# Softmax weights split on the query side and transposed by DMA in a two-layer GLA and dilated-attention trunk

## The chip, the cores and the metric

The kernel runs on one core of one Trainium2 chip. The metric is the device time of one execution in microseconds (us), as a median of several runs. All times below are us unless ns is written.

## What is computed

The reference runs two pre-norm residual layers over 2048 tokens of width 1024. Layer A mixes with gated linear attention, layer B with dilated window attention in three groups of six heads; both add a four-head attention into a memory of 256 tokens. The two places with a softmax are what matters here:

```python
def memory_attention(q, mem_n, w_memkv):          # 4 heads of 64, 256 memory tokens
    s = jnp.einsum('bthd,bnhd->bhtn', q, k).astype(jnp.float32) * (MEM_HEAD_DIM ** -0.5)
    p = jax.nn.softmax(s, axis=-1).astype(v.dtype)
    o = jnp.einsum('bhtn,bnhd->bthd', p, v)

def dilated_group(q, k, v, window, dilation):     # 6 heads of 128, blocks of 128 queries
    s = jnp.einsum('bphjqd,bphjkd->bphjqk', qb, kw).astype(jnp.float32) * (Dh ** -0.5)
    s = jnp.where(mask, s, -jnp.inf)              # own block and the one before it
    m = jnp.max(s, axis=-1, keepdims=True)
    p = jnp.exp(s - m)
    den = jnp.sum(p, axis=-1, keepdims=True)
    o = jnp.einsum('bphjqk,bphjkd->bphjqd', (p / den).astype(v.dtype), vw)
    lse = (m + jnp.log(den))[..., 0]
```

## The kernel before

Every product runs on TensorE (PE) in fp16 halves: a number is kept as a high half and a low half, and `mm3` (L164) makes three matmuls, high by high, high by low, low by high. The program is written in straight line; a scheduler sets the order on each engine, so code of one step stands between code of others. All DMAs are issued by SyncE (SP) on one queue.

Layer A has two loops over 16 blocks of 128 tokens. The first does the linear attention. The second does, for each block, `a2_q` (queries of the memory attention, its scores and its weighted sum, L612), `a2_gate` (96 matmuls of the gate path), `a2_branch` and `a2_out` (96 matmuls of the output projection) and `a2_h2`. Layer B runs over nine units (three pairs of heads, three groups). A unit projects queries and keys (`proj_qk`, eight tiles of 24 matmuls of 512 columns for each head), values (`proj_v`), and calls `attend` (L819) once for each of its two heads. Between and after the units stand `gate_item`s (24, L923), which join the three groups' outputs, and at the end comes the memory attention of layer B over 16 blocks (`mem_scores` one block ahead of `mem_pv`). An output projection closes the kernel.

The softmax path is the same in both places. Scores land in a PSUM bank with queries on partitions. VectorE (DVE) takes the maximum (L833 in `attend`, L243 in `mem_scores`), ScalarE (ACT) makes the exponentials into an fp32 tile in SBUF (L844, tile `pm`; L249, tiles `mp` and `mpt`). The weighted sum needs keys on partitions, so PE transposes each 128x128 block (L847; L161 in `split_T`), ACT copies the PSUM result to fp16 with the factor SP = 2**14 (L852, L262), DVE writes the remainder (L853, L263) and PE multiplies by the values (L165 to L167 into `ps_o`; L271 and L273). `attend` works on pairs of query blocks, eight pairs for each head. In it a pair has 2 to 4 blocks of weights to transpose: 31, 28 and 16 blocks for each head in the three groups, 450 in all; the two memory attentions have 8 for each token block, 256 in all. Tiles of the pool `bk` have two buffers, those of `gk` one. The staging tiles `stg` (pools `stg` and `sga`, one buffer each) hold raw weights while they are split.

Of the kernel before, what the change touches and what calls it, by code (L numbers as in the profile page):

```python
# [26 lines left out]
SQ = 2.0 ** -16  # L27
SP = 2.0 ** 14
NEG = -3.0e38
GROUPS = ((1, 16), (4, 4), (16, 1))  # L30
# [3 lines left out]
def trunk(ctx, tc, a, out):  # L34
# [23 lines left out]
    def bank(p_):  # L58
        return tl(p_, [P, 512], F32, p_.name)

# [1 line left out]
    def cload(name, shape, dt=F32, src=None):  # L62
# [93 lines left out]
    def split_T(src, n, emit):  # L156
        for k0 in range(0, n, 4):
# [15 lines left out]

# [1 line left out]
    def mem_kv(i, memT, spools):  # L175
# [26 lines left out]
    def load_mem(i, pl, invs, iq):  # L202
        kk = tl(pl, [P, 4, 256], F16, f"kk{i}")
        kl = tl(pl, [64, 4, 256], F16, f"kl{i}")
        vm = tl(pl, [P, 2, 512], F16, f"vm{i}")
        for hh in range(2):
            for dst, j in ((kk[0:64], 0), (kk[64:128], 0), (kl, 1)):
                SY.dma_start(dst.rearrange("p (r h) n -> p h r n", h=2)[:, hh],
                             kv_d[i][j, hh * 64:(hh + 1) * 64, :].rearrange("p (r n) -> p r n", r=2))
        SY.dma_start(vm, kv_d[i][2:4].rearrange("j p n -> p j n"))  # L210
        sc = col()
        V.tensor_scalar(out=sc, in0=iq, scalar1=invs[0], scalar2=0.125 / SQ, op0=ALU.mult, op1=ALU.mult)
        ov = col()
        V.tensor_scalar(out=ov, in0=invs[1], scalar1=1.0 / SP, scalar2=None, op0=ALU.mult)
        return kk, kl, vm, sc, neg_of(sc), ov
# [8 lines left out]

    def mem_scores(mem, q2, wk, tg):
        kk, kl, vm, sc, nsc, ov = mem
        qmT = tl(wk, [P, 512], F16, tg[0])
        t = tl(ps_tr, [P, 1024], F16, "ps_tr")
        for j in range(4):
            PE.transpose(t[:, j * P:(j + 1) * P], q2[:, j].rearrange("p a d -> p (a d)"), id16)  # L230
        V.tensor_copy(qmT, t[:, :512])
        den = tl(sp, [P, 4], F32, "mden")
        mx = tl(sp, [P, 4], F32, "mmx")
        ps = []
        for hh in range(2):
            s = bank(ps_g)
            for jj in range(2):
# [6 lines left out]
            V.tensor_scalar(out=m2, in0=m2, scalar1=nsc, scalar2=None, op0=ALU.mult)  # L244
            p_ = tl(wk, [P, 512], F32, tg[1 + hh])
            ps.append(p_)
            for jj in range(2):
                j = hh * 2 + jj
                A.activation(out=p_[:, jj * 256:(jj + 1) * 256], in_=s[:, jj * 256:(jj + 1) * 256],  # L249
                             func=AF.Exp, scale=sc, bias=m2[:, jj:jj + 1], accum_out=den[:, j:j + 1])  # L250
        return ps, den

    def mem_pv(mem, sd, om, po):
# [4 lines left out]
        for hh in range(2):  # L258
            pt = ps[hh].bitcast(F16).rearrange("p (a n) -> p a n", a=2)

            def emit2(k0, k1, t, pt=pt):
                A.activation(out=pt[:, 0, :], in_=t, func=AF.Copy, scale=SP)  # L262
                V.scalar_tensor_tensor(out=pt[:, 1, :], in0=t, scalar=SP, in1=pt[:, 0, :], op0=ALU.mult,  # L263
                                       op1=ALU.subtract)
            split_T(ps[hh], 4, emit2)
            for jj in range(2):
                j = hh * 2 + jj
                for m in range(2):
                    ts = slice((jj * 2 + m) * P, (jj * 2 + m + 1) * P)
                    vs = slice(m * 256 + j * 64, m * 256 + (j + 1) * 64)  # L270
                    PE.matmul(ov2[:, :, j * 64:(j + 1) * 64], pt[:, 0, ts], vm[:, :, vs], start=m == 0,  # L271
                              stop=False)
                    PE.matmul(ov2[:, 0, j * 64:(j + 1) * 64], pt[:, 1, ts], vm[:, 0, vs], start=False,  # L273
                              stop=m == 1)
# [37 lines left out]

    # =============== layer A ===============
    pa_ctx = ctx.enter_context(ExitStack())
# [284 lines left out]
    with ExitStack() as c2:  # L599
# [12 lines left out]
        def a2_q(b):  # L612
# [92 lines left out]

    # =============== layer B ===============
    turn = [0]
# [23 lines left out]
    bk = c3.enter_context(pool("bk", 2))  # L731
    c4 = c3.enter_context(ExitStack())
    cb = c4.enter_context(pool("cb", 1))
    masks = {}
# [21 lines left out]
    def load_v(u, cps=None):  # L756
        base = wbase(u)
        wv, iv = load_w256(w_in_b[:, base + 1536:base + 1792], invh1, wp, None, cps)
        f = col()
        V.tensor_scalar(out=f, in0=iv, scalar1=1.0 / (SQ * SP), scalar2=None, op0=ALU.mult)  # L760
        fsc[u] = f
        return wv
# [48 lines left out]
    def attend(u, i, qk, vts, w_):  # L811
# [6 lines left out]
        for j4 in range(4):  # L818
            ob = bank(ps_o)  # L819
            for j2 in range(2):  # L820
                js = [j4 * 4 + j2 * 2, j4 * 4 + j2 * 2 + 1]
                s = bank(ps_g)
                mx = tl(sp, [P, 2], F32, "mx")
                pm = tl(bk, [P, 512], F32, "pm")
                ws = []
                for jj, j in enumerate(js):
                    w = 2 if j % nb > 0 else 1
                    ws.append(w)
                    o = s[:, jj * 256:jj * 256 + w * P]
# [3 lines left out]
                    V.tensor_tensor_reduce(out=pm[:, jj * 256:jj * 256 + w * P], in0=o,  # L833
                                           in1=masks["mw" if w == 2 else "mf"], scale=1.0,
                                           scalar=NEG, op0=ALU.add, op1=ALU.max,
                                           accum_out=mx[:, jj:jj + 1])
                V.tensor_scalar(out=st[:, js[0]:js[0] + 2], in0=mx, scalar1=nsc, scalar2=None, op0=ALU.mult)  # L837
                pt = bank(ps_tr)
                slot = 0
                slots = []  # L840
                for jj, j in enumerate(js):
                    w = ws[jj]
                    p_ = pm[:, jj * 256:jj * 256 + w * P]
                    A.activation(out=p_, in_=p_, func=AF.Exp, scale=sc, bias=st[:, j:j + 1],  # L844
                                 accum_out=st[:, 16 + j:17 + j])
                    for hf in range(w):
                        PE.transpose(pt[:, slot * P:(slot + 1) * P], p_[:, hf * P:(hf + 1) * P], ident)  # L847
                        slots.append((jj, hf, slot))
                        slot += 1
                ptf = tl(bk, [P, 2, 512], F16, "pt")  # L850
                n = slot * P
# [12 lines left out]
                for r_, (kb, sl, n, j) in enumerate(runs):  # L864
                    vt = vts[kb // 8]
                    cs = slice(sl * P, (sl + n) * P)
                    mm3(ob[:, j * P:(j + n) * P], vt[:, 0, kb % 8, i * P:(i + 1) * P],
                        vt[:, 1, kb % 8, i * P:(i + 1) * P], ptf[:, 0, cs], ptf[:, 1, cs],
                        j2 == 0 and r_ == 0, j2 == 1 and r_ == len(runs) - 1)
# [55 lines left out]
    def gate_item(hp, w_, c, i, ep):  # L925
# [108 lines left out]
    def mem_a(p_):  # L1034
        return mem_scores(mem1, mem_q(mk, wm, p_), mk, ("qmT", "mp", "mpt"))

    sd = mem_a(0)
    for p_ in range(NB):
        c = p_ // 4
        if p_ % 4 == 0:  # L1040
            onats[c] = [tl(bk, [P, 2, 256], F32, ("pm", "pt")[c % 2]) for _ in range(2)]
        sn = mem_a(p_ + 1) if p_ + 1 < NB else None
# [17 lines left out]

    # =============== output projection and final norm ===============
    with ExitStack() as c5:
# [102 lines left out]
```

## Time and profile before

| | us |
|---|---|
| median of 3 runs (2763.5 to 2766.29) | 2764.64 |
| span of the profiled execution | 2762.3 |
| PE busy | 2699.6 (98%) |
| DVE, ACT, POOL busy | 1592.6, 1121.6, 270.6 |
| second loop of layer A, from about | 460 to 900 |
| the nine units of layer B, from about | 966 to 2399 |
| memory attention of layer B, from about | 2399 to 2555 |

The profile names the span alone for its own execution; the three runs lie 1.2 to 4.0 above it. The page gives the busy time of each engine; the timeline gives each instruction with its start and length; the lines view groups equal instructions; the waits view says for whom an engine stood idle; the chain of waits follows the work that ended last back in time. Matmuls are pipelined: their lengths overlap, and the distance from one start to the next is the pace.

### The profile page before, as it was taken

Reading aid. Unit: us, or ns where it says so; the run is one execution under the profiler, and the core shown is the slowest. Engines: PE = TensorE matmul, PEld = TensorE weight load, DVE = VectorE, ACT = ScalarE, POOL = GpSimd, SP = SyncE. Lnnn points to the kernel's source line nnn. Section 1 sums busy time; section 2 is a strip of 40 time slices with the busy share of each in tenths; the row PEclk is TensorE's granted clock in tenths of the full one; section 3 lists DMA queues with packets and bytes.
Section 4 is the critical chain, followed back from the end, with each engine's and each line's share of the span. In section 5 each row is a group of like instructions: output and inputs, shape, how many; then the busy total and the mean of one; then the engine's idle time right before and its main releaser. Section 6 shows DMA issues by size and latency. Waiting matters only on the chain.

```text
span 2762.3 us, 49951 instructions
## 1 busy us (share of the span) xinstructions
PE 2699.6 (98%) x20616; PEld 2048.7 (74%) x20616; DVE 1592.6 (58%) x3557; ACT 1121.6 (41%) x2621; POOL 270.6 (10%) x211
## 2 busy tenths in 40 slices
PE   7999999999999999999999999999999999899999
PEld 6889998888888856858575575766667584556899
DVE  6345445655655467373757738556664737776433
ACT  6356445534434434242425324233433424444322
POOL 0000000000000021010211212111110103220000
PEclk9999999999999999999999999999999999999999
DMA  5242112221211211010211332011111114662432
GB/s 200 92 138 99 64 51 100 79 79 59 78 68 51 80 35 47 20 56 15 66 45 62 85 94 91 23 43 57 50 40 35 39 38 117 180 162 64 137 139 107
DMA packets 190152, 213.06 MB, mean 77 GB/s; under 512 B 63282, under 2 KB 153060, under 8 KB 189924
## 3 DMA queue, kind: packets, MB, share of 16 engines
q1 hardware_dynamic: 189924, 209.88, 23.6%
q8 instruction: 161, 2.64, 0.4%
q14 instruction: 67, 0.55, 0.1%
HBM read 149.63 MB, written 60.21 MB: 76 GB/s over the span
## 4 chain that ended last, share of the span: by engine, by line
PE 84%; DVE 5%; DMA 5%; ACT 2%; POOL 1%; issue 1%; SPq 1%; DVEq 0%; POOLq 0%; ACTq 0%
PE ps_mm L165 15%; PE ps_mm L167 15%; PE ps_mm L166 15%; PE ps_x L165 6%; PE ps_x L167 6%; PE ps_x L166 6%; DMA fb<-fd 3%; PE ps_tr L161 2%; PE ps_o L165 2%; PE ps_o L167 2%; PE ps_o L166 2%; PE ps_tr L847 2%; PE ps_mm L187 1%; PE ps_g L165 1%; PE ps_g L166 1%
## 5 line engine op out<-in xcount | busy, mean ns | idle before, releaser
L165 PE MATMUL ps_mm<-w,hT 128*128 128x256 f16 (+1 forms) x1408 | 385.8, 274 | 4.0 <-DVE qm L221 1.7
L166 PE MATMUL ps_mm<-w,hT 128*128 128x256 f16 (+1 forms) x1408 | 384.6, 274 | 0.0
L167 PE MATMUL ps_mm<-w,hT 128*128 128x256 f16 (+1 forms) x1408 | 383.8, 274 | 0.4 <-DVE hT L364 0.4
L802 POOL TENSOR_TENSOR sh<-sh,rope 32x512 f32<-32x512 f32 x144 | 183.2, 1273 | 1892.4 <-DVE sh L801 1892.1
L165 PE MATMUL ps_mm<-h2T,w 128*128 128x512 f16 x944 | 359.7, 381 | 0.9 <-ACT w L133 0.8
L166 PE MATMUL ps_mm<-h2T,w 128*128 128x512 f16 x944 | 359.4, 381 | 0.0
L167 PE MATMUL ps_mm<-h2T,w 128*128 128x512 f16 x944 | 359.0, 381 | 0.0
L167 PEld LDWEIGHTS <-w 128*128 128x128 f16 x1408 | 139.1, 99 | 140.7 <-issue 2.7
L166 PEld LDWEIGHTS <-w 128*128 128x128 f16 x1408 | 138.4, 98 | 139.0 <-issue 4.1
L165 PEld LDWEIGHTS <-w 128*128 128x128 f16 x1408 | 138.6, 98 | 138.2 <-issue 2.1
L166 PE MATMUL ps_mm<-w,h2T 128*128 128x256 f16 x840 | 229.2, 273 | 0.0
L167 PE MATMUL ps_mm<-w,h2T 128*128 128x256 f16 x840 | 229.2, 273 | 0.0
L165 PE MATMUL ps_mm<-w,h2T 128*128 128x256 f16 x840 | 229.1, 273 | 0.0
L844 ACT ACTIVATE pm<-pm,st,cols 128x256 f32<-128x256 f32 (+1 forms) x288 | 156.4, 544 | 162.2 <-DVE st L837 161.9
L165 PE MATMUL ps_x<-h2T,w 128*128 128x512 f16 x464 | 176.6, 381 | 2.3 <-DVE q L807 1.9
L166 PE MATMUL ps_x<-h2T,w 128*128 128x512 f16 x464 | 176.4, 380 | 0.0
L167 PE MATMUL ps_x<-h2T,w 128*128 128x512 f16 x464 | 176.4, 380 | 0.0
L166 PEld LDWEIGHTS <-h2T 128*128 128x128 f16 x1280 | 149.2, 117 | 8.2 <-issue 0.7
L165 PEld LDWEIGHTS <-h2T 128*128 128x128 f16 x1280 | 149.1, 116 | 8.0 <-DVE qm L221 0.3
L166 PEld LDWEIGHTS <-hT 128*128 128x128 f16 x1408 | 138.2, 98 | 22.5 <-issue 4.8
L165 PEld LDWEIGHTS <-hT 128*128 128x128 f16 x1408 | 138.6, 98 | 21.6 <-issue 2.1
L167 PEld LDWEIGHTS <-h2T 128*128 128x128 f16 x1280 | 149.2, 117 | 5.7
(338 smaller groups left out, 6336.0 us busy)
## 6 DMA issues: line engine op xcount, KB each, us to landing
stg<-in_w_in_b SPq DMA_DIRECT2D x64, 512.0 KB
od<-osb SPq DMA_DIRECT2D x72, 256.0 KB
og<-od SPq DMA_DIRECT2D x72, 256.0 KB
fb<-fd SPq DMA_DIRECT2D x24, 768.0 KB
x<-in_x SPq DMA_DIRECT2D x32, 512.0 KB
hTd<-hT SPq DMA_DIRECT2D x16, 512.0 KB
hT<-hTd SPq DMA_DIRECT2D x16, 512.0 KB
x1d<-x SPq DMA_DIRECT2D x16, 512.0 KB
```

The source lines that it names most:

```text
L161: PE.transpose(t[:, (k - k0) * P:(k - k0 + 1) * P], src[:, k * P:(k + 1) * P], ident)
L165: PE.matmul(o, sh, mh, start=first, stop=False)
L166: PE.matmul(o, sh, ml, start=False, stop=False)
L167: PE.matmul(o, sl, mh, start=False, stop=last)
L187: PE.matmul(t[:, m * 256:(m + 1) * 256], w[:, k, ms] if j == 0 else memT[:, k, ms], memT[:, k, :] if j == 0 else w[:, k, :], start=k == 0, ...
L802: G.tensor_tensor(out=sw, in0=sw, in1=rs, op=ALU.mult)
L844: A.activation(out=p_, in_=p_, func=AF.Exp, scale=sc, bias=st[:, j:j + 1], accum_out=st[:, 16 + j:17 + j])
L847: PE.transpose(pt[:, slot * P:(slot + 1) * P], p_[:, hf * P:(hf + 1) * P], ident)
```

## The change

The weights are split before they are transposed. ScalarE copies the fp32 exponentials to fp16 in SBUF, GpSimd (POOL) writes the remainder beside them, and one DMA transpose, issued by SP, moves both halves (up to eight 128x128 blocks of fp16) into a second tile with keys on partitions. That takes the place of the PE transposes, the ACT copy out of PSUM and the DVE remainder. The factor SP moves into the exponent as a summand LSP.

```diff
+    def split_P(src, n, hl, pt):
+        fl = hl.rearrange("p a n -> p (a n)")
+        hi, lo = fl[:, :n], fl[:, n:2 * n]
+        A.activation(out=hi, in_=src, func=AF.Copy)
+        G.tensor_tensor(out=lo, in0=src, in1=hi, op=ALU.subtract)
+        SY.dma_start_transpose(pt[:, :2 * n // P, :], fl[:, :2 * n])
+        pf = pt.rearrange("p a n -> p (a n)")
+        return pf[:, :n], pf[:, n:2 * n]
...
# mem_scores and mem_pv
+            hl = tl(hls[hh][0], [P, 2, 512], F16, hls[hh][1])
+            ps.append(split_P(p_, 512, hl, p_.bitcast(F16).rearrange("p (a n) -> p a n", n=P)))
...
-            def emit2(k0, k1, t, pt=pt):
-                A.activation(out=pt[:, 0, :], in_=t, func=AF.Copy, scale=SP)
-                V.scalar_tensor_tensor(out=pt[:, 1, :], in0=t, scalar=SP, in1=pt[:, 0, :], op0=ALU.mult,
-                                       op1=ALU.subtract)
-            split_T(ps[hh], 4, emit2)
...
-            mem_pv(mem0, mem_scores(mem0, qm, k2, ("qmT", "mp", "mpt")), om, ps_g)
+            mem_pv(mem0, mem_scores(mem0, qm, k2, ("qmT", "mp", "mpt"), ((stg, "stg"), (sga, "stg"))), om, ps_g)
...
# attend
-                pm = tl(bk, [P, 512], F32, "pm")
+                pm = tl(pk, [P, 512], F32, "pm")
...
-                    for hf in range(w):
-                        PE.transpose(pt[:, slot * P:(slot + 1) * P], p_[:, hf * P:(hf + 1) * P], ident)
...
-                A.activation(out=ptf[:, 0, :n], in_=pt[:, :n], func=AF.Copy, scale=SP)
-                V.scalar_tensor_tensor(out=ptf[:, 1, :n], in0=pt[:, :n], scalar=SP, in1=ptf[:, 0, :n],
-                                       op0=ALU.mult, op1=ALU.subtract)
+                pth, ptl = split_P(pm[:, :at], at, tl(pk, [P, 2, 512], F16, "ph"),
+                                   tl(pk, [P, 8, P], F16, "pt"))
...
# gate_item
-        og = tl(bk, [P, 3, 512], F32, "og")
+        og = tl(gk, [P, 3, 512], F32, "og")
```

In layer A the fp16 halves use the staging tiles, which hold raw weights at other times; in layer B they have tiles of their own. `og`, the three groups' outputs of one `gate_item`, goes from two buffers to one.

The scheduler orders the changed program anew. On ScalarE in the second loop of layer A the rows of one block's memory attention read before (`mp` and `mpt` are the two halves of the heads, `e` is the gate's exponential, `ps_tr` the bank with PE's transposes):

```order
L249 ACTIVATE mp_6932,mden_6923<-ps_g_6925,mmx_6924,cols_88 128x256 x2
L249 ACTIVATE mpt_6942,mden_6923<-ps_g_6935,mmx_6924,cols_88 128x256 x2
L262 ACTIVATE mp_6932<-ps_tr_6946 128x512
L289 ACTIVATE e_7088<-e_7088 128x512
L262 ACTIVATE mpt_6942<-ps_tr_6961 128x512
L290 ACTIVATE e_7088<-e_7088,cols_88 128x512
L291 ACTIVATE e_7088<-e_7088 128x512
```

And of the changed program (lines are counted from its own file):

```order
L258 ACTIVATE mp_6902,mden_6893<-ps_g_6895,mmx_6894,cols_88 128x256 x2
L258 ACTIVATE mpt_6916,mden_6893<-ps_g_6909,mmx_6894,cols_88 128x256 x2
L168 ACTIVATE stg_6905<-mp_6902 128x512
L168 ACTIVATE stg_6919<-mpt_6916 128x512
L294 ACTIVATE e_7052<-e_7052 128x512
L295 ACTIVATE e_7052<-e_7052,cols_88 128x512
L296 ACTIVATE e_7052<-e_7052 128x512
```

Both copies stand right behind the exponentials and no longer behind PE's transposes. On SP the same stretch reads before (`hT`, `x`, `og` are loads of a block, `x1d` its store):

```order
L614 DMA hT_7254<-hTd_11_99 128x2048
L659 DMA x_7108<-in_x 128x1024
L640 DMA og_7235<-ogd_26_114 128x768
L668 DMA x1d_125<-x_6739 128x1024
L614 DMA hT_7623<-hTd_12_100 128x2048
```

And of the changed program:

```order
L619 DMA hT_7581<-hTd_12_100 128x2048
L170 DMA_TRANSPOSE mp_6902<-stg_6905 128x8x128
L170 DMA_TRANSPOSE mpt_6916<-stg_6919 128x8x128
L664 DMA x_7435<-in_x 128x1024
L645 DMA og_7562<-ogd_27_115 128x768
L673 DMA x1d_125<-x_7072 128x1024
```

The two transposes stand one behind the other on the one queue, and the loads of the next blocks behind them. On SP in the memory attention of layer B, around one `gate_item`, the rows read before (`brd` is the store of an item's result, `fb` its factors, `og` the groups' outputs of a later item):

```order
L949 DMA brd_71_159<-sg_26562 512x1x128
L931 DMA fb_26713<-fd_67_155 128x1536
L934 DMA og_27257<-od_0_53_141 128x512
L935 DMA og_27257<-od_1_54_142 128x4x128
L936 DMA og_27257<-od_2_55_143 128x16x32
L949 DMA brd_71_159<-sg_26706 512x1x128
```

And of the changed program:

```order
L951 DMA brd_70_158<-sg_25752 512x1x128
L933 DMA fb_26151<-fd_66_154 128x1536
L1071 DMA w_27284<-brd_69_157 128x1024
L936 DMA og_26291<-od_0_53_141 128x512
L937 DMA og_26291<-od_1_54_142 128x4x128
L938 DMA og_26291<-od_2_55_143 128x16x32
L170 DMA_TRANSPOSE mp_26098<-mh_3164_26101 128x8x128
L170 DMA_TRANSPOSE mpt_26112<-mh_3167_26115 128x8x128
L951 DMA brd_71_159<-sg_26144 512x1x128
```

Here the transposes stand behind the loads of `og`, and those wait until GpSimd and DVE are done with the one buffer of the item before.

## Rows read from the trace of the kernel before

**Rows 1.** The page, part 1: busy us, share of span and instructions of each engine

```profile
PE 2699.6 (98%) x20616; PEld 2048.7 (74%) x20616; DVE 1592.6 (58%) x3557; ACT 1121.6 (41%) x2621; POOL 270.6 (10%) x211
```

**Rows 2.** By stage: busy PE, PEld, DVE, ACT, POOL (instructions), clock, DMA share, GB/s

```profile
460.00:900.00 440.00, 437.74 (x4075) 383.92 (x4074) 266.91 (x600) 197.10 (x435) 0.00 (x0) 1.00 0.21 72
966.00:1500.00 534.00, 534.00 (x3664) 351.01 (x3663) 326.55 (x787) 194.47 (x455) 82.99 (x65) 1.00 0.13 42
1500.00:1690.00 190.00, 179.81 (x1139) 113.09 (x1138) 112.13 (x218) 63.12 (x128) 42.09 (x27) 0.98 0.32 91
1690.00:2270.00 580.00, 579.35 (x4150) 399.25 (x4150) 338.99 (x834) 211.87 (x503) 79.37 (x63) 1.00 0.13 41
2270.00:2399.00 129.00, 118.19 (x726) 64.77 (x725) 99.07 (x215) 59.18 (x140) 35.68 (x22) 0.97 0.54 157
2399.00:2555.00 156.00, 148.78 (x1071) 93.96 (x1070) 114.61 (x233) 76.66 (x197) 27.57 (x16) 0.97 0.39 109
```

**Rows 3.** PE timeline, second loop of layer A: start us, length us, instruction

```profile
705.17 0.27 PE L167 MATMUL ps_x<-wo,bT 128*128 128x256 f16 x1
705.28 1.04 PE L161 MATMUL ps_tr<-ident,sg 128*128 128x128 f32 x8
706.15 0.27 PE L166 MATMUL ps_mm<-w,hT 128*128 128x256 f16 x1
```

**Rows 4.** Lines by form: PE's transposes of weights, count, busy us, mean ns

```profile
L847 PE MATMUL ps_tr<-ident,pm 128*128 128x128 f32 x450 | 90.5, 278 | 3.5 <-ACT pm L844 3.1
L161 PE MATMUL ps_tr<-ident,mp 128*128 128x128 f32 x128 | 23.7, 284 | 2.8 <-ACT mp L249 1.9 <-DVE qmT L231 0.9
```

**Rows 5.** Lines by form: DVE remainder, an ACT pass over SBUF, POOL on two inputs

```profile
L853 DVE SCALAR_TENSOR_TENSOR pt<-ps_tr,pt 128x512 f16<-128x512 f32 x66 | 45.3, 687 | 9.3 <-ACT pt L852 8.7
L289 ACT ACTIVATE e<-e 128x512 f32<-128x512 f32 x64 | 40.2, 629 | 124.1 <-DVE e L287 123.2 <-DVE stok L98 0.9
L802 POOL TENSOR_TENSOR sh<-sh,rope 32x512 f32<-32x512 f32 x144 | 183.2, 1273 | 1892.4 <-DVE sh L801 1892.1
L942 POOL TENSOR_TENSOR fb<-og,fb 128x512 f32<-128x512 f32 x24 | 40.0, 1665 | 0.0
```

**Rows 6.** Timeline, one block of layer A: last scores on PE, last exponential on ACT

```profile
713.65 0.28 PE L241 MATMUL ps_g<-kl,qmT 64*128 64x256 f16 x1
716.98 0.21 ACT L249 ACTIVATION_READ_ACCUMULATOR mpt<-ps_g,mmx,cols 128x1 f32 x1
```

**Rows 7.** Timeline, one pair of attend: last scores on PE, last exponential on ACT

```profile
1046.76 0.27 PE L167 MATMUL ps_g<-k,q 128*128 128x256 f16 x1
1049.96 0.18 ACT L844 ACTIVATION_READ_ACCUMULATOR pm<-pm,st,cols 128x1 f32 x1
```

**Rows 8.** Chain of waits: start us, us, transfers that were waited for

```profile
929.79 6.87 DMA stg<-in_w_in_b
2358.20 5.89 DMA fb<-fd
2383.00 1.76 DMA std<-stT
2420.26 2.88 DMA brd<-sg
```

**Rows 9.** PE's waits: who waited for whom, us, times, longest

```profile
PE ps_o L166 <- DVE pt L853: 5.0, 6, 2.7
```

**Rows 10.** DMA view of 1064 to 1076: GB/s in 40 slices, and the issue

```profile
GB/s 0 0 0 0 0 0 0 27 123 181 253 276 379 389 379 389 389 382 290 38 0 0 0 0 0 0 0 0 0 0 0 0 0 0 0 0 0 0 0 0
stg<-in_w_in_b SPq DMA_DIRECT2D x2, 512.0 KB
```

**Rows 11.** SP's timeline, one gate item: factors, a later item's outputs, next factors

```profile
2446.25 0.57 SPq L931 DMA_DIRECT2D fb<-fd  x1
2454.38 0.33 SPq L934 DMA_DIRECT2D og<-od  x1
2458.63 0.56 SPq L931 DMA_DIRECT2D fb<-fd  x1
```

More of the change, by code (lines that the diff above doesn't have):

```diff
@@ L28 @@
 SP = 2.0 ** 14
+LSP = math.log(SP)
 NEG = -3.0e38
@@ L213, in load_mem @@
         ov = col()
-        V.tensor_scalar(out=ov, in0=invs[1], scalar1=1.0 / SP, scalar2=None, op0=ALU.mult)
+        V.tensor_copy(ov, invs[1])
         return kk, kl, vm, sc, neg_of(sc), ov
@@ L243, in mem_scores @@
             V.tensor_reduce(out=m2, in_=s.rearrange("p (a b) -> p a b", a=2), axis=AX.X, op=ALU.max)
-            V.tensor_scalar(out=m2, in0=m2, scalar1=nsc, scalar2=None, op0=ALU.mult)
+            V.tensor_scalar(out=m2, in0=m2, scalar1=nsc, scalar2=LSP, op0=ALU.mult, op1=ALU.add)
             p_ = tl(wk, [P, 512], F32, tg[1 + hh])
-            ps.append(p_)
             for jj in range(2):
@@ L270, in mem_pv @@
                     vs = slice(m * 256 + j * 64, m * 256 + (j + 1) * 64)
-                    PE.matmul(ov2[:, :, j * 64:(j + 1) * 64], pt[:, 0, ts], vm[:, :, vs], start=m == 0,
+                    PE.matmul(ov2[:, :, j * 64:(j + 1) * 64], pth[:, ts], vm[:, :, vs], start=m == 0,
                               stop=False)
-                    PE.matmul(ov2[:, 0, j * 64:(j + 1) * 64], pt[:, 1, ts], vm[:, 0, vs], start=False,
+                    PE.matmul(ov2[:, 0, j * 64:(j + 1) * 64], ptl[:, ts], vm[:, 0, vs], start=False,
                               stop=m == 1)
@@ L759, in load_v @@
         f = col()
-        V.tensor_scalar(out=f, in0=iv, scalar1=1.0 / (SQ * SP), scalar2=None, op0=ALU.mult)
+        V.tensor_scalar(out=f, in0=iv, scalar1=1.0 / SQ, scalar2=None, op0=ALU.mult)
         fsc[u] = f
@@ L823, in attend @@
                 mx = tl(sp, [P, 2], F32, "mx")
-                pm = tl(bk, [P, 512], F32, "pm")
+                pm = tl(pk, [P, 512], F32, "pm")
                 ws = []
+                at = 0
+                slots = []
                 for jj, j in enumerate(js):
@@ L832, in attend @@
                     mm3(o, q[:, 0, qs], q[:, 1, qs], k_[:, 0, ks], k_[:, 1, ks], True, True)
-                    V.tensor_tensor_reduce(out=pm[:, jj * 256:jj * 256 + w * P], in0=o,
+                    slots += [(jj, hf, at // P + hf) for hf in range(w)]
+                    V.tensor_tensor_reduce(out=pm[:, at:at + w * P], in0=o,
                                            in1=masks["mw" if w == 2 else "mf"], scale=1.0,
@@ L836, in attend @@
                                            accum_out=mx[:, jj:jj + 1])
[L837 to L840, printed above, removed]
+                    at += w * P
+                V.tensor_scalar(out=st[:, js[0]:js[0] + 2], in0=mx, scalar1=nsc, scalar2=LSP, op0=ALU.mult,
+                                op1=ALU.add)
+                at = 0
                 for jj, j in enumerate(js):
[L842 to L843 removed]
+                    p_ = pm[:, at:at + ws[jj] * P]
+                    at += ws[jj] * P
                     A.activation(out=p_, in_=p_, func=AF.Exp, scale=sc, bias=st[:, j:j + 1],
                                  accum_out=st[:, 16 + j:17 + j])
[L846 to L854 removed]
+                pth, ptl = split_P(pm[:, :at], at, tl(pk, [P, 2, 512], F16, "ph"),
+                                   tl(pk, [P, 8, P], F16, "pt"))
                 runs = []
@@ L1034, in mem_a @@
     def mem_a(p_):
-        return mem_scores(mem1, mem_q(mk, wm, p_), mk, ("qmT", "mp", "mpt"))
+        return mem_scores(mem1, mem_q(mk, wm, p_), mk, ("qmT", "mp", "mpt"), ((mk, "mh0"), (mk, "mh1")))
     sd = mem_a(0)
@@ L1040, in trunk @@
         if p_ % 4 == 0:
-            onats[c] = [tl(bk, [P, 2, 256], F32, ("pm", "pt")[c % 2]) for _ in range(2)]
+            onats[c] = [tl(mk, [P, 2, 256], F32, ("om0", "om1")[c % 2]) for _ in range(2)]
         sn = mem_a(p_ + 1) if p_ + 1 < NB else None
```

9 lines of the change are left out of this document (5 added, 4 removed).

## The prediction, written before the changed kernel was run

> **What bounds the kernel now.** I read the page's busy times first, then the same by stage, then PE's timeline. PE is busy 2699.6 of 2762.3 us [rows 1]. By stage it is full where the change works: 437.74 of 440 in layer A's second loop, 534 of 534 and 579.35 of 580 in two long stretches of layer B [rows 2]. Only where `gate_item`s run (1500 to 1690, 2270 to 2399, 2399 to 2555) it idles 10, 11 and 7 us. DVE is at 58 to 77% in layer B, ACT at 36 to 49%, POOL below 30%. PE's waits name the weights' path for 5.0 us in six waits [rows 9]: today that path is hidden. So a matmul taken from PE is worth its slot, as long as what takes its place arrives before PE comes to need it.
>
> **What is removed.** A matmul of 256 columns starts 0.11 us behind the one before it, and eight transposes fill 705.28 to 706.15, 0.109 each [rows 3]; the 273 to 284 ns of one that the lines view gives overlap. There are 450 in `attend` and two times 128 in the memory attentions [rows 4]: 706 x 0.109 = **77.0 us off PE**, 49.1 in `attend`, 14 in each memory attention. DVE loses 208 remainders of up to 0.687 us [rows 5]. ACT's copy stays: 0.63 from SBUF, going by a pass over SBUF of the same size [rows 5]. These two engines don't bound these stages, so I count nothing for them.
>
> **What is added.** For each of 208 tiles of weights: a POOL subtraction, an SP issue, and a transposing transfer of 256 KB or less. Copy and subtraction run beside PE; they cost only if the path from scores to weighted sum grows longer than the PE work placed between the two. That work I counted in the built order and priced by [rows 3].
>
> Layer A: between a block's last scores and its first weighted sum stand 89 matmuls of 256 columns, 89 x 0.109 = 9.7 us; the half `mpt` follows 0.6 later, so 10.3. The path: last scores end at 713.93, last exponential at 717.19 [rows 6], so 3.3; then two copies of 0.63. POOL's subtraction is not in the trace: 1.27 for 512 elements on 32 partitions, 1.67 on 128 with strided reads [rows 5]. I take 1.27, as its data lie in one piece, and keep 1.67. The first subtraction starts behind the first copy at 3.9 and the second ends at 3.9 + 2 x 1.27 = 6.4. That leaves 10.3 - 6.4 = 3.9 for the transfer of `mpt`.
>
> Attend: between a pair's last scores and its weighted sum stand 10.4 us of PE work at the median of the 144 pairs, 8.8 at the shortest tenth, 5.6 at the shortest. The path: 1047.03 to 1050.14 [rows 7] is 3.1, plus 0.63, plus 1.27, is 5.0 without the transfer. Summing over the pairs what a path of length C exceeds the work between (less delay already taken inside that stretch) gives 6 us at C = 8, 16 at 9, 26 at 9.5, 42 at 10, 129 at 12, 184 at 13. Layer B's memory attention has more room: 1 at 9, 9 at 12.
>
> **The transfer** decides, and the trace has none like it. I call T its time from SP's issue until PE may start. Transfers that PE's chain waited for took 1.76 (2 KB in short pieces), 2.88 (256 KB from SBUF in pieces of 512 bytes), 5.89 (768 KB) and 6.87 (the first of a weight's loads) [rows 8]. Nearest by size and source is 2.88; the pieces of a transpose are finer and two are issued back to back, so I take **4.0**, and keep 2.9 and 6.9 for the range. With 4.0: layer A is 0.1 to 0.3 late, 3 us in 16 blocks. Attend has C = 9.0; where ACT or DVE is busy it is 9.5; between 16 and 26 I take 21. Layer B's memory attention: 1.
>
> [...]
>
> **What else moves.** (1) All transfers go through one queue. A weight's load holds it 3.6 us at up to 389 GB/s [rows 10]; three for each of nine units, with a pair of blocks every 10 us (144 in 966 to 2399), catch a transfer some 10 times for 1.8 on average, 17 us, some of it inside the slack: 10, between 0 and 17. (2) In layer A the staging tiles now carry the halves, so the four loads of the output weights and the first of layer B's weights go behind the memory attention instead of ahead of it. The order leaves 28 us of PE work before the first use; cover is there, the price is one or two late row sums: 6, between 0 and 20. (3) `gate_item`: one cycle from `fb` to `fb` takes 12.4 us (2446.25 to 2458.63), and the outputs `og` of a later item are fetched inside it, at 2454.38 [rows 11]. With one buffer they are fetched behind the factors; SP's next transposes wait behind those loads, and POOL's next subtractions behind products that wait for the factors. At 1.5 more for each of 24 items, half of it seen by PE: 18, between 0 and 48.
>
> **Sum.** 2764.6 - 77.0 + 3 + 21 + 1 + 10 + 6 + 18 = **2747** (the sum is made on the profiled span of 2762.3, which lies 2.3 under the median; that difference is kept). Its own range, with T from 3.3 to 4.7, is 2715 to 2760.
>
> **Rivals.** *All hidden:* T = 2.9 or less, and the queue as free as DMA's share of 0.13 in the long stretches says [rows 2]. 2764.6 - 77 + 6 + 4 = 2698. Against it: fine pieces, one queue.
>
> *The transfer comes late (slower):* PE waits for the transposed weights where it now waits for nobody. Break-even: stalls of 77 - 34 = 43 in the two attentions, reached at T = 4.7 (layer A 13, attend 32). At T = 6.9, the longest row, layer A waits 16 x 3.0 = 48, attend (C = 11.9) 124, layer B's memory 8: 2764.6 - 77 + 180 + 34 = 2902. For it: SP takes both transposes of a block one after the other, and the room in layer A is 3.9. Against: PE has work in front of every weighted sum.
>
> *Blocks one after another:* if each 128x128 block is a small transfer of its own at 1.76, eight take 14.1: 163 + 538 + 72 of stalls, 3495. For it: the order shows the destination as eight blocks; against: 512 pieces of one store take 2.88 together [rows 8]. [...]
>
> *The gate items take it back:* the transfers are in time, but the cycle of 12.4 grows by 2.5 on the 16 items that run from 2270 on, where PE already idles 18 us: 40 in place of 18, 2769, no change.
>
> **Chances.** The forecast 0.36, all hidden 0.12, gate items 0.12, late transfer 0.28, block by block 0.12. Range: 2698 to 2900, which leaves out the last and little else. A measurement of this kernel tells 0.2%, 5.5 us, from no change. Faster: 0.36 and 0.12 less the forecast's upper edge, 0.46. Same: that edge and most of the gate items, 0.12. Slower: late, block by block and the rest, 0.42.
>
> **What would show it.** 706 fewer transposes on PE and 77 us less of PE's busy time show the removal. The transfer is read from SP's issue of a transpose to the first weighted sum that waited for it: under 4.7 the forecast stands, over it PE's waits name that transfer with tens of us, in layer A's blocks first. If POOL's subtraction takes 1.7 or more, the room shrinks by 0.4 in attend and 0.8 in layer A. If the stretch from 2270 to 2555 grows while the long stretches shrink, the gate items took it. I am wrong if PE idles in the long stretches for someone other than the transfer, or if DVE's lighter load moves the time.

## The result, and the profile after

The changed kernel takes 2730.43 us (median of four runs, 2728.72 to 2734.91) beside 2765.06 of the kernel before on the same chip: a ratio of 0.9875, 95% interval 0.9863 to 0.9887, 34.6 us faster. The forecast was 2747 and faster. The profiled execution, with a span of 2733.0, is the longest of the four; sums on spans therefore show 29.3 us where the medians show 34.6.

The page, part 1 (busy us, share, instructions), answering to [rows 1]:

```profile
PE 2630.3 (96%) x19910; PEld 1971.7 (72%) x19910; DVE 1511.4 (55%) x3349; ACT 1129.3 (41%) x2621; POOL 494.5 (18%) x419
```

706 matmuls fewer, as forecast; PE's busy time falls by 69.3 and not by 77.0 (at a granted clock of 0.50 a matmul of 256 columns is 0.42 us long, last section, and 0.27 in [rows 3]). By stage, over the same times as [rows 2] (busy PE, PEld, DVE, ACT, POOL, clock, DMA share, GB/s):

```profile
460.00:900.00 440.00, 432.65 (x3974) 375.56 (x3973) 252.77 (x576) 200.51 (x431) 37.11 (x32) 0.98 0.33 96
966.00:1500.00 534.00, 526.91 (x3560) 335.67 (x3558) 310.10 (x760) 201.90 (x471) 142.90 (x124) 1.00 0.25 65
1690.00:2270.00 580.00, 572.47 (x4036) 381.90 (x4035) 326.00 (x801) 222.56 (x525) 152.64 (x133) 1.00 0.28 70
2270.00:2399.00 129.00, 108.64 (x678) 59.62 (x677) 94.43 (x185) 61.99 (x147) 43.95 (x32) 0.95 0.64 164
2399.00:2555.00 156.00, 138.28 (x981) 86.80 (x979) 104.71 (x178) 73.96 (x177) 56.50 (x38) 0.96 0.64 152
```

Idle time of PE (window less busy) went from at most 1 us to 7 in each of the two long stretches of layer B, from 2 to 7 in layer A's second loop, and from 18 to 38 between 2270 and 2555. Who it waits for, in PE's waits (us, times, longest):

```profile
PE ps_o L175 <- DMA pt<-ph: 20.6, 17, 3.6
PE ps_tr L240 <- DVE qm L231: 10.5, 9, 2.4
...
PE ps_g L175 <- DVE mx L842: 7.7, 11, 1.6
...
PE ps_o L276 <- DMA mp<-mh: 5.2, 2, 4.7
...
PE ps_g L276 <- DMA mpt<-stg: 3.3, 2, 3.0
```

`pt<-ph` is attend's transfer; the waits of [rows 9] are gone. To see where the 29.3 us came from I read the same three instructions in both traces: the last ACT copy into `h2T` (layer A ends), the last copy of `attend`'s output, and the last scaling of layer B's memory attention. Before:

```profile
928.03 1.09 ACT L679 ACTIVATE h2T<-ps_tr 128x512 f16<-128x512 f32 x2 [1.28 <-PE ps_tr L161]
2385.10 0.69 DVE L871 COPY osb<-ps_o 128x512 f32<-128x512 f32 x1
2580.97 0.42 DVE L280 TENSOR_TENSOR pt<-pt,mden 128x256 f32<-128x256 f32 x1
```

And after:

```profile
926.18 1.08 ACT L684 ACTIVATE h2T<-ps_tr 128x512 f16<-128x512 f32 x2 [1.53 <-PE ps_tr L162]
2351.34 0.68 DVE L873 COPY osb<-ps_o 128x512 f32<-128x512 f32 x1
2552.89 0.42 DVE L285 TENSOR_TENSOR om<-om,mden 128x256 f32<-128x256 f32 x1
```

| part | slots freed | time gained | lost | forecast of the loss |
|---|---|---|---|---|
| to the end of layer A | 14.0 | 928.03 - 926.18 = 1.9 | 12.1 | 3 + 6 |
| units, to the last `attend` | 49.1 | 33.8 - 1.9 = 31.9 | 17.2 | 21 + 10 |
| to the end of layer B's memory attention | 14.0 | 28.1 - 33.8 = -5.7 | 19.7 | 1 + 18 |
| output projection | 0 | 29.3 - 28.1 = 1.2 | -1.2 | 0 |

The gate items lie in the second and third parts: SP loads the factors of 15 of the 24 before the last `attend` and of 9 behind it, so the 18 in the table's third line belongs to both. Traces of kernels with the same layer A differ by up to 3.5 us there (gains of 1.9, 3.7, 4.4 and 5.3), so single entries are good to a few us.

### The profile page after: what moved, and what is told of

Same layout as the page of the kernel before. It is cut to its first block, busy times and chain, and to the rows that moved or that the text cites. A ratio compares the mean times of both kernels' runs of the same rounds, so it can differ in the third digit from the quotient of the medians.

```text
span 2733.0 us, 49414 instructions
## 1 busy us (share of the span) xinstructions
PE 2630.3 (96%) x19910; PEld 1971.7 (72%) x19910; DVE 1511.4 (55%) x3349; ACT 1129.3 (41%) x2621; POOL 494.5 (18%) x419
## 5 line engine op out<-in xcount | busy, mean ns | idle before, releaser
L169 POOL TENSOR_TENSOR ph<-pm,ph 128x512 f16<-128x512 f32 (+2 forms) x144 | 143.5, 1001 | 292.0 <-issue 158.9
L169 POOL TENSOR_TENSOR stg<-mp,stg 128x512 f16<-128x512 f32 x16 | 18.5, 1156 | 850.0 <-DMA ogd<-og 460.3
L176 PEld LDWEIGHTS <-h2T 128*128 128x128 f16 x1280 | 149.8, 117 | 11.1 <-issue 3.1
L176 PEld LDWEIGHTS <-hT 128*128 128x128 f16 x1408 | 139.1, 99 | 24.6 <-issue 6.0
L175 PEld LDWEIGHTS <-h2T 128*128 128x128 f16 x1280 | 150.0, 117 | 8.6 <-issue 0.2
```

The source lines that it names most:

```text
L169: G.tensor_tensor(out=lo, in0=src, in1=hi, op=ALU.subtract)
```

## The experiments

Each ran beside the kernel before, and each ratio is to that. For every run the same three instructions were read; the table gives us against the trace of the kernel before, negative for earlier.

| kernel | layer A | last attend | memory attention | span | median us |
|---|---|---|---|---|---|
| changed | -1.9 | -33.8 | -28.1 | -29.3 | 2730.4 |
| e1 attend alone | +0.3 | -32.7 | -30.9 | -31.7 | 2735.6 |
| e2 memory attentions alone | -1.4 | +2.1 | +0.1 | +0.7 | 2763.9 |
| e3 no transfers | -3.5 | -45.5 | -49.2 | -46.7 | 2717.4 |
| e4 transfers twice | +9.2 | +2.5 | +24.3 | +22.0 | 2793.1 |
| e5 loads first | -4.8 | -38.6 | -33.0 | -32.8 | 2729.2 |
| e6 two `og` | -4.4 | -36.9 | -32.1 | -32.8 | 2730.6 |
| e7 two `fb` | -3.7 | -38.5 | -47.6 | -48.8 | 2715.7 |
| e8 before, two `fb` | +1.2 | +2.4 | +8.7 | +0.7 | 2762.9 |
| e9 one staging tile | -2.9 | -34.9 | -43.4 | -44.6 | 2720.0 |
| e10 weights on ACT's queue | -5.3 | -38.8 | -35.1 | -36.3 | 2734.0 |
| e11 subtraction on DVE | +11.6 | -19.2 | -8.9 | -8.5 | 2755.1 |
| e12 two `fb`, loads first | -2.4 | -40.5 | -47.4 | -48.4 | 2715.8 |

### One part alone

```diff
# e1: both memory attentions as before
-            ps.append(split_P(p_, 512, hl, ...))
+            split_T(ps[hh], 4, emit2)
# e2: attend as before
-                pth, ptl = split_P(pm[:, :at], at, ...)
+                        PE.transpose(pt[:, slot * P:(slot + 1) * P], p_[:, hf * P:(hf + 1) * P], ident)
```

> The changed kernel with both memory attentions as they were before (PE transposes, ACT copy, DVE remainder), og with two buffers and the staging tiles free of halves; attend as changed. Theory (what the two traces show: attend saves 450 slots, 49 us, loses 20.6 us to PE waits for the transposed weights, and gets back 8 us of waits that PE had there before): 2762.3 - 49 + 20.6 - 8 = 2726 us of span, 36 us less than before, so as fast as the fully changed kernel or up to 9 us faster. Rival (the prediction's own terms: attend's stalls 21 and the shared queue 10 more): 2764.6 - 49 + 31 = 2747. Rival (the gain came from the memory attentions): about 2760.

Measured: 2735.58, ratio 0.9899 [0.9885, 0.9914], 29 us faster. The span fell by 31.7; the 2747 made from the prediction's terms falls outside. The theory's 36 was too much. It had added up waits named in the profile as if each came back whole; that this is the reason is argued and not shown here.

> The counterpart: attend as it was before, both memory attentions as changed, og with one buffer, layer A's halves in the staging tiles. Theory: the two memory attentions save 28 us of PE slots and lose 12 us in layer A's first blocks (two idle stretches and the half clock behind them) and 21 us around the gate items, so 2765 + 5 = 2770 us, between 2765 and 2775: slower than before or the same. Rival (the prediction's terms: 3 + 1 + 6 + 18 = 28 us lost): 2765, no change. Rival (the stalls of the fully changed kernel came from attend's transfers on the shared queue): 28 us gained less 9, 2746.

Measured: 2763.89, ratio 0.9995 [0.9986, 1.0005]: no change. 28 us of PE slots freed bring nothing by themselves. What the change gains is `attend`'s; with both parts it is 5 us more than with `attend` alone, about what these medians can tell apart.

### The transfers left out, and done twice

```diff
# e3
-        SY.dma_start_transpose(pt[:, :2 * n // P, :], fl[:, :2 * n])
+        return hi, lo
# e4
+        SY.dma_start_transpose(pt[:, :2 * n // P, :], fl[:, :2 * n])
```

> The fully changed kernel without the transposing transfers: PE reads the untransposed halves, so the weighted sums are of the wrong entries; copies, subtraction, buffers and the moved loads stay. Theory (the transfer is what PE waits for in attend, and one of several things around the gate items): the 20.6 us of attend's waits, 3 in layer A and 7 in layer B's memory attention go, 2730 - 30 = 2700. Rival (all that was lost was lost to the transfers): the 77 us of PE slots less nothing, 2765 - 77 = 2688, plus the 8 us of old waits, 2680. Rival (the losses are in subtraction, buffers and loads, and the transfer is hidden): 2725.

Measured: 2717.39, ratio 0.9831 [0.9814, 0.9847]. PE reads halves that were not transposed, so this bounds the time and is no version of the kernel. All 208 transfers together cost 2730.4 - 2717.4 = 13 us by the medians; by the traces 1.6 in layer A, 10.1 in the units, 9.4 behind them, less 3.7 in the output projection. The time lies between the theory's 2700 and the 2725 of a hidden transfer. PE's waits named the transfers for 20.6 + 5.2 + 3.3 us and more, but with the transfers gone others came last in their place (PE's waits, kernel without transfers):

```profile
PE ps_g L173 <- DVE mx L840: 9.1, 14, 1.8
PE ps_o L276 <- POOL mh L169: 7.8, 6, 2.8
PE ps_o L174 <- POOL ph L169: 5.5, 6, 2.0
```

It also shows that "all hidden" at 2698 was out of reach for this program: with nothing to hide, it stands at 2717.

> The fully changed kernel with each transposing transfer issued twice in a row (same source, same destination). One transfer holds SP for 1.23 us and its data are with PE 3.7 to 4.5 us after its issue began; twice adds at least 1.2 us and at most 4. Theory (the length of attend's path decides, as the count of PE work between scores and weighted sum gives it: 16 us at C = 9.0, 42 at 10, 129 at 12): at 2.5 us more C is 11.5, the stalls of attend grow by about 90 us, layer A's by 16 x 2, so 2730 + 120 = 2850, between 2790 and 2900. Rival (PE's order leaves more room than the count says): under 2760.

Measured: 2793.08, ratio 1.0101 [1.0086, 1.0116]: 63 us slower than the changed kernel, between the two. The second transfer writes the tile of the first, and SP waits for the first to land before it issues it. SP's waits (us, times, longest):

```profile
SPq L171 <- DMA pt<-ph: 108.8, 86, 5.8
```

One pair on SP (L170 is the first, L171 the second; other DMAs stand between):

```profile
1760.10 1.30 SPq L170 DMA_TRANSPOSE pt<-ph  x1
1762.91 1.24 SPq L171 DMA_TRANSPOSE pt<-ph  x1
```

And on PE:

```profile
1765.67 0.22 PE L176 MATMUL ps_o<-pt,v 128*128 128x128 f16 x1 [1.00 <-DMA pt<-ph]
```

The second issue stands 2.8 us behind the first and PE starts 2.8 us behind the second, 5.6 in all. The trace also has the time at which each transfer set its semaphore: over the 144 pairs of `attend` the second lands 6.0 us (median) after the issue of the first, where a single one of the changed kernel takes 2.8 (below). That is 3.2 more, over the 2.5 that I had taken. In the units this lost 2.5 - 9.2 - (-31.9) = 25 us against the changed kernel. Between C = 7.8 and 11.0 the count behind the prediction grows by some 80 (an estimate between its values), so the count, made on the order before, gives PE less room than it has. The longer way of the weights turned a gain of 35 us into a loss of 28; but SP also stands still while it waits for the first of a pair and everything behind it with it, and what each of the two costs was not separated.

### The loads of the output weights

What happens at 460 to 500 in layer A of the changed kernel, by stretches of 10 us (columns as above):

```profile
465.00:475.00 10.00, 7.13 (x69) 6.12 (x67) 2.58 (x7) 6.90 (x16) 1.16 (x1) 1.00 0.83 156
475.00:485.00 10.00, 8.87 (x63) 7.25 (x64) 5.25 (x16) 4.78 (x10) 0.00 (x0) 0.66 0.49 161
485.00:495.00 10.00, 8.54 (x78) 7.44 (x77) 7.38 (x13) 8.32 (x16) 0.00 (x0) 1.00 0.70 228
495.00:505.00 10.00, 8.47 (x54) 6.92 (x54) 7.79 (x20) 6.88 (x13) 0.00 (x0) 0.66 0.34 105
```

and the same four stretches before:

```profile
465.00:475.00 10.00, 7.84 (x79) 6.79 (x77) 7.75 (x21) 9.60 (x21) 0.00 (x0) 1.00 0.18 55
475.00:485.00 10.00, 10.00 (x95) 9.00 (x94) 8.24 (x19) 8.11 (x14) 0.00 (x0) 1.00 0.73 250
485.00:495.00 10.00, 9.91 (x94) 8.72 (x92) 9.20 (x16) 7.79 (x14) 0.00 (x0) 1.00 0.50 157
495.00:505.00 10.00, 10.00 (x86) 8.26 (x85) 6.52 (x20) 3.49 (x10) 0.00 (x0) 1.00 0.15 41
```

PE idles 7.0 us in place of 2.3, and a granted clock of 0.66 in a stretch of 10 us, made up of 1.00 and of the 0.50 measured from 476 to 481 and from 496 to 502, means 6.8 us at half clock and 3.4 us lost, twice. 4.7 + 6.8 = 11.5 us: nearly all that layer A lost. PE stood first for a row sum of output weights, then for the first block's `mpt`:

```profile
472.80 0.38 PE L124 MATMUL ps_tr<-rm,ones 128*128 128x1 f32 x2 [1.05 <-ACT wo L121]
476.13 0.29 PE L276 MATMUL ps_g<-vm,mpt 128*128 128x128 f16 x1 [2.96 <-DMA mpt<-stg]
```

On SP:

```profile
467.80 0.95 SPq L112 DMA_DIRECT2D stg<-in_w_out  x2
468.85 1.24 SPq L170 DMA_TRANSPOSE mpt<-stg  x1
```

The transpose stands behind 1 MB of weights in the one queue and takes 7.3 us (468.85 to 476.13); the other 31 of layer A landed 2.7 to 4.1 us after their issue. Nearly all of layer A's loss is made here: the last copy of the first block into `h2T` comes 14 us later than before, that of the second 11, and most of the later blocks then gain 0.9 us each, which is their eight slots. Without the transfers the first block is still 7.6 us late. Two kernels tried to move this:

```diff
# e5: loads written first
-        hT, om = a2_q(0)
         for j in range(4): ... load_w(wt, [(0, a["w_out"][0, :, j * 256:(j + 1) * 256])], ...)
+        hT, om = a2_q(0)
```

> The fully changed kernel with the loads of layer A's output weights written ahead of the first block's memory attention, so that on SP they come before its transposes. In the changed kernel the second loop of layer A falls 11 us behind at 460 to 500 and then gains 15 us; without the transfers (run e3_no_transfer) it still falls 6 us behind there. Theory (the loads that wait for the staging tiles cost it, by two idle stretches of PE and the half clock after each): the 11 us go, 2730 - 10 = 2720, between 2715 and 2724. Rival (it is the first transposes that are late, behind whatever load): 2730, no change. Rival (the first block's halves now wait for the staging tiles): slower than 2733.

Measured: 2729.17, ratio 0.9861 [0.9842, 0.9881]; the changed kernel's 0.9875 lies in that interval. PE no longer waits there for a transfer, but for row sums of the output weights, behind ACT's work on `wo` (PE's waits at 460 to 500):

```profile
PE ps_tr L124 <- ACT wo L121: 5.6, 2, 5.2
```

```diff
# e9: with two fb (below); both halves in one staging tile
-            hl = tl(hls[hh][0], [P, 2, 512], F16, hls[hh][1])
+            hl = both[:, 2 * hh:2 * hh + 2, :]      # both = tl(sga, [P, 4, 512], F16, "stg")
```

> The kernel of run e7_two_fb with both halves of layer A's weights in one of the two staging tiles (the other holds them no more), so that the first load of the output weights and the first of layer B's go ahead of the transposes again. Theory (the loads that wait for a staging tile cost the changed kernel up to 11 us at 460 to 500; with the loads simply written first, run e5_loads_first, 7 us were still lost, since the first block then waited in its turn): at least half of that comes back, 2716 - 6 = 2710, between 2704 and 2713. Rival (the scheduler's place for the row sums of the output weights on PE costs it, whatever tile): 2716, no change. Rival (one tile for both halves makes each block's transposes wait for the other half): over 2720.

Measured: 2719.95, ratio 0.983 [0.9813, 0.9846], no better than 0.9817 of the run it builds on. PE still idles 9.6 us between 460 and 500. So neither the order of the loads nor the tile alone is the cause; that the place of the row sums on PE is, was not tried.

### The gate items

```diff
# e6: og from gk to bk (two buffers); layer B's halves and qmT with one buffer
# e7, e8: fb instead
-        fb = tl(gk, [P, 3, 16, 32], F32, "fb")
+        fb = tl(bk, [P, 3, 16, 32], F32, "fb")
# e8 on the kernel before, with og from bk to gk
```

> The fully changed kernel with two buffers for og again, as before the change (the room comes from one buffer in place of two for layer B's halves and the transposed queries). The stretch from the last unit's first gate item to the end of layer B's memory attention takes 301.6 us before and 310.5 after, with 14 us of PE slots removed in it: about 23 us lost. Rival by the prediction (the one buffer of og carries much of the 18 us it counted for the gate items): 2730 - 12 = 2718. Theory (one cycle from factors to factors takes 12.8 us before, 13.3 without the transfers and 15.7 with them, so it is the transposes on SP ahead of the next load of factors, not og): no change, 2727 to 2733.

Measured: 2730.6, ratio 0.9877 [0.9854, 0.9899]: no change. But the cycle did become shorter. SP's loads of `fb`, changed kernel, first and last of a row of six:

```profile
2380.36 0.34 SPq L933 DMA_DIRECT2D fb<-fd  x1
...
2458.15 0.62 SPq L933 DMA_DIRECT2D fb<-fd  x1
```

And the same six in the kernel with two `og`:

```profile
2376.07 0.52 SPq L933 DMA_DIRECT2D fb<-fd  x1
...
2444.42 0.63 SPq L933 DMA_DIRECT2D fb<-fd  x1
```

Five cycles take 77.8 us in the one, 15.6 each, and 68.4 in the other, 13.7 each (before, 12.4 in [rows 11] and 12.8 over the five cycles from 2420.97). So `og` did lengthen the cycle, which my expectation denied, and the cycle by itself does not set the time, which it had taken for granted. This run also takes one of the two buffers from layer B's halves, and what that costs was not run by itself; run e7_two_fb takes the same one and gains 15 us all the same.

> The fully changed kernel with two buffers for the factors fb of a gate item (room as in the run with two og), og with one. Theory (the stretch is bound by the chain of one buffer: load of 5.2 us, products, sums, store, then transposes of the memory attention on SP ahead of the next load; PE idles 42 us in it): with the next factors fetched meanwhile the stretch of 310 us shrinks toward PE's own work of 268, by 20 to 35 us: 2730 - 27 = 2703. Rival (PE there waits for the transposed weights of the memory attention itself, 7 us, and for DVE): 2723. Rival (a second buffer brings more loads ahead of the transposes on SP): 2730 or more.

Measured: 2715.66, ratio 0.9817 [0.9799, 0.9835]: 15 us better than the changed kernel and, with the run e12_fb_and_loads, the fastest that was found. From the last `attend` to the end of the memory attention it takes 186.8 us in place of 201.6 (195.9 before).

> The kernel before with two buffers for fb and one for og, nothing else. Theory (the gate cycles bound that stretch already before the change, PE idling 18.5 us in it, so that 14 us less of PE's work there could not be collected): the idle time goes, 2765 - 15 = 2750, between 2745 and 2757. Rival (PE binds that stretch before the change): 2765, no change. Rival (one buffer of og costs what two of fb give): 2765 or more.

Measured: 2762.92, ratio 0.9988 [0.9979, 0.9998], under 0.2% and so no change; the theory falls. (The mark of the memory attention's end lies 8.7 us later in this trace and the span is only 0.7 longer, because more of the output projection runs ahead of that mark; it is no measure of the stretch here.) Yet freeing PE alone gains nothing there either (e2: 193.9 for 195.9). That fits a stretch in which PE's work and the gate items' chain were about equally long before the change, so that either alone buys nothing and both together do; it is argued from these four runs and not shown by one of its own.

The edits of the runs e5_loads_first and e7_two_fb together:

> Two edits together on the fully changed kernel: two buffers for the factors fb (run e7_two_fb, 2716 us) and layer A's output weights written ahead of the first memory attention (run e5_loads_first, in whose trace the fall at 460 to 500 is 6.3 us in place of 10.8, while its median of 2729 is within the scatter of the changed kernel's 2730). Theory (the two losses lie in different stretches and add): 2716 - 4 = 2712, between 2708 and 2716. Rival (what the loads gain at 460 to 500 is lost at the seam to layer B or is scatter): 2716 to 2720.

Measured: 2715.8, ratio 0.982 [0.9806, 0.9834]. That is where the theory's range ends and the rival's begins; beside the 2715.7 of run e7_two_fb the loads written first add nothing, as the rival has it.

### The queue, and the engine of the subtraction

```diff
# e10: load_w of layer B
-                SY.dma_start(raw[:, k0:k0 + 4, c0:c0 + m], v[:, k0:k0 + 4, :])
+                A.dma_start(raw[:, k0:k0 + 4, c0:c0 + m], v[:, k0:k0 + 4, :])
# e11: split_P
-        G.tensor_tensor(out=lo, in0=src, in1=hi, op=ALU.subtract)
+        V.tensor_tensor(out=lo, in0=src, in1=hi, op=ALU.subtract)
```

> The fully changed kernel with layer B's weight loads issued by ScalarE on its own queue, so that they no longer stand in the queue of the transposes. Rival by the prediction (loads that hold the one queue cost attend 10 us): 2730 - 10 = 2720. Theory (attend lost 11 us to the transfers in all, of which the loads are the few waits that follow one): 2730 - 4 = 2726, between 2722 and 2731. Rival (ScalarE now waits for staging tiles in front of its exponentials, or the two queues share the same engines and only interleave): slower, 2735 to 2760.

Measured: 2734.01, ratio 0.988 [0.9863, 0.9897]: no gain. The units take 33.6 us less than before, beside 31.9 with one queue. Taking the loads out of the queue gave back none of the 10 us that I had counted for it. Nor did the transfers come sooner: 15 of `attend`'s 144 landed more than 4.7 us after their issue, and 19 with one queue. How the transfers of the two queues share the engines was not measured, so the rival that they interleave was not ruled out.

> The fully changed kernel with the subtraction on VectorE in place of GpSimd. GpSimd takes 1.16 us for 512 elements, VectorE some 0.6 to 0.7. Theory (path length decides in attend and the gate items share GpSimd with the subtraction): each path is 0.5 us shorter, by the count of PE work 5 us less stall, and the gate items' products no longer stand ahead of it: 2730 - 8 = 2722. Rival (VectorE is the busiest engine beside PE, 58 to 77% in layer B, and each subtraction then stands behind others there): no change to 15 us slower, 2730 to 2745.

Measured: 2755.08, ratio 0.9957 [0.9942, 0.9972]: 25 us slower than with GpSimd, though one subtraction is shorter. GpSimd's in the changed kernel, then DVE's (lines by form: count, busy us, mean ns, idle before):

```profile
L169 POOL TENSOR_TENSOR ph<-pm,ph 128x512 f16<-128x512 f32 x66 | 79.5, 1208 | 119.5 <-ACT ph L168 70.5 <-issue 37.8 <-DMA pt<-ph 6.1
```

On DVE:

```profile
L169 DVE TENSOR_TENSOR ph<-pm,ph 128x512 f16<-128x512 f32 x66 | 48.9, 746 | 23.8 <-ACT ph L168 23.5
```

By the table 13.5 of the 20.8 us between the two spans are lost in layer A, 1.1 in the units, 4.6 in the memory attention and 1.6 after it. In layer A the waits for the transposed weights that the change had kept to two (3.3 us, above) become eight:

```profile
PE ps_g L276 <- DMA mpt<-stg: 4.8, 8, 2.6
```

These waits grew by 1.5 us and do not make up the 13.5: the first block is 3.8 us later, and from the third to the eleventh each gains 0.3 us, beside 0.8 with GpSimd. The subtraction itself is not late there (SP's issue follows the end of the copy by 0.8 and 1.6 us for the two halves at the median, beside 1.3 and 2.1 with GpSimd), but the transfers land 4.7 and 4.4 us after their issue at the median, beside 3.6 and 3.4. Nothing else is written differently, yet the scheduler orders anew, on DVE as on SP. So the choice of the engine was worth 25 us; how much of that is DVE's load, the place in DVE's order or SP's new order was not separated.

## Why the prediction was right, and where its terms were off

**Removal.** 706 slots went, 77.0 us as counted; by the spans 47.7 of them were lost again, by the medians 42.4. I had put 59.

**The transfer, T.** Taken as 4.0 from SP's issue to PE. Two waits for it, issue and matmul (2 us ahead of the first went a load of weights, ahead of the second a store):

```profile
1672.17 1.23 SPq L170 DMA_TRANSPOSE pt<-ph  x1
```

PE:

```profile
1676.70 0.22 PE L175 MATMUL ps_o<-pt,v 128*128 128x128 f16 x1 [1.87 <-DMA pt<-ph]
```

And again, SP:

```profile
1480.13 1.30 SPq L170 DMA_TRANSPOSE pt<-ph  x1
```

PE:

```profile
1484.54 0.22 PE L175 MATMUL ps_o<-pt,v 128*128 128x128 f16 x1 [1.38 <-DMA pt<-ph]
```

That is 4.5 and 4.4: over my value, under the 4.7 at which I had put the break-even. But these are transfers that PE had to wait for, and so the late ones. Here is one of eight blocks that shares its time with no other, on SP:

```profile
1995.14 1.23 SPq L170 DMA_TRANSPOSE pt<-ph  x1
```

The DMA view of 1995 to 1999 counts 1056 packets for it, all under 512 B, 0.26 MB together, so its pieces are finer than those of 512 B in the store of [rows 8]. GB/s in 40 slices of 0.1 us:

```profile
GB/s 0 0 0 0 0 0 0 0 0 0 0 0 0 95 256 289 289 294 289 289 289 287 206 39 0 0 0 0 0 0 0 0 0 0 0 0 0 0 0 0
```

Its data have moved 2.3 us after the issue began, and its semaphore is set at 2.75. By the semaphores of all 144 in `attend` the median is 2.75, from 2.3 to 7.4; 32 took over 4.0 and 19 over 4.7. One that PE waited for:

```profile
2239.34 1.22 SPq L170 DMA_TRANSPOSE pt<-ph  x1
```

PE:

```profile
2245.48 0.22 PE L175 MATMUL ps_o<-pt,v 128*128 128x128 f16 x1 [0.85 <-DMA pt<-ph]
```

6.1 us. So one T for all transfers was the wrong picture: the usual one takes 2.8 and is in time, and PE waits for a few late ones. Of the 32 over 4.0, 16 shared their time with a load of weights, of the other 112 only 18; that the loads delay them is argued, and run e10_weights_on_scalar_queue shows that another queue does not help. The usual 2.75 is close to the nearest regular row, 2.88 from its issue on [rows 8]; in GB/s it is lower, 289 here beside 389 in [rows 10]. Eight blocks within 2.8 us also rule out the rival "block by block", which had 14.1 for them (the transfer of 1.76 that it counted eight times moved 8 KB, in the DMA view of 2380 to 2386 of the kernel before, and not 2).

**The path ahead of it.** ACT's copy was put at 0.63; 66 of 512 columns took 0.62 on average. The subtraction was put at 1.27; its mean in `attend` was 1.21 above, well under the 1.7 that would have shrunk the room (in layer B's memory attention it was 1.32 to 1.41). Both steps stand.

**Attend and the queue, 21 + 10.** This is the step that failed in size: 17.2 lost in the units, the gate items there included, and 10.1 of it to the transfers (run e3_no_transfer). As far as the times to landing tell, the two terms count the same lateness twice. The 21 came from a T of 4.0 for every pair; with the usual 2.8 the prediction's own count gives under 6, and its 10 for transfers that are caught behind others then stands for the late ones. PE's waits do name 20.6 us, but when the transfers were taken away PE waited for DVE and GpSimd instead and half of it stayed. I had also given no credit for the 8.1 us of waits on the old path in the trace before ([rows 4, 9]).

**Layer A, 3 + 6.** 12.1 lost. The place was right (the loads moved behind the memory attention, priced at one or two late row sums). What the step left out is that a granted clock of 0.50 came behind the idle time here: 4.7 us of idle time more, 6.8 us of clock. The 3 for a late transfer in every block did not come; behind 505 PE's waits name it for 0.4 us. Why PE idles at the start of the loop stays open, since with the loads or the halves moved (runs e5_loads_first, e9_one_staging_tile) PE still idles 8.0 and 9.6 us there.

**Memory attention and gate items, 1 + 18.** 19.7 lost behind the last `attend`. The size looks right and is luck: the 18 was for 24 items, and 9 of them run there, 7 us by my price. The reason does not stand either. I had named the single `og`; with two of them the cycle shortens and the time stays. A second `fb` gives 15 us back.

**DVE's relief, counted at nothing.** In doubt, by my own mark ("if DVE's lighter load moves the time"): with the subtraction on DVE the time is 2755, a gain of 10 us in place of 35. That run changes the orders on DVE and SP too, so what the relief alone was worth is not measured. I had looked for whether DVE bounds the stage (61% busy in layer A, 266.91 of 440 in [rows 2]) and not for who stands behind it in its order.

**Rivals.** The late transfer came for 19 of `attend`'s 144 and not for all; with two in a row (run e4_transfer_twice) the kernel did become slower, as that rival has it. The cycle of the gate items grew by 2.8 us, to 15.6 over five of them from 12.8, more than the 2.5 of the rival at 2769, but the last part lost 19.7 and not 40: the cycle alone does not set the time.

**The sum.** It came 17 us too high. By the spans 11 of these are errors of the terms: `attend` and the queue 14 too much, layer A 3 and the memory attention 1 too little, the output projection 1 not counted; the rest is that the profiled execution is the longest of the four. With the regular row's 2.88 for T (a stall of 6 in `attend` and none in layer A) the sum would have been 2747 - 15 - 3 = 2729, beside 2730.4. That, too, is closer than its parts, which miss layer A by 6 us. The range said for T from 3.3 to 4.7 does not follow from the prediction's terms either: at 4.7 they give 2764.6 - 77 + 13 + 32 + 1 + 34 = 2768 and not 2760.

## What to carry over

Slots taken from a full engine did not come back in full here: 49 us freed in the units gave 32, while 28 freed in the two memory attentions gave nothing by themselves. Read the length of the new path against the work in front of its end, and the spread of that length rather than one value; a duration taken only from what was waited for was too long here (4.4 and 4.5, beside 2.8 at the median). Then ask which engine does its steps and who queues behind them there; here the subtraction on GpSimd was worth 25 us, although one of 512 columns took 1.21 us there and 0.75 on DVE. Don't add up named waits as if removing their cause gave them back: 20.6 us were named in `attend` and 10 came back in the units.

## What the runs showed that was not expected

The stalls of PE at 460 to 500 cost more than their length. Behind the wait that ended at 476.13 PE's timeline of the changed kernel reads:

```profile
476.96 0.42 PE L176 MATMUL ps_mm<-w,hT 128*128 128x256 f16 x1
477.17 0.42 PE L177 MATMUL ps_mm<-w,hT 128*128 128x256 f16 x1
```

and the stretch of 2 us behind it:

```profile
478.00:480.00 2.00, 2.00 (x12) 1.42 (x10) 1.67 (x5) 0.00 (x0) 0.00 (x0) 0.50 1.07 338
```

Matmuls of 256 columns start 0.21 us apart in place of 0.11 [rows 3], PE counts as fully busy, and the granted clock is 0.50; at 465 to 475, before the wait, it was 1.00. A transposing transfer usually holds SP for 1.2 to 1.3 us at its issue (above; up to 3.4), where a store of 256 KB takes

```profile
1046.79 0.33 SPq L874 DMA_DIRECT2D od<-osb  x1
```

and the 208 of them hold it for 292 us. And DMA's share in the two long stretches of layer B doubles, 0.13 to 0.25 and 0.28.
